# Hybrid encoder step on one core: feed-forward order, means of squares, transposed keys and first norm tiles

## The chip, the cores and the metric

The kernel runs on one NeuronCore of a Trainium2 chip. Its time is the device time of one launch in microseconds (us), as a median over runs. The engines have separate instruction queues and each works its queue in order: TensorE (PE) multiplies, VectorE (DVE) and ScalarE (ACT) work element by element and read the accumulators in PSUM, GpSimd (POOL) helps in SBUF and issues transfers, SyncE (SP) issues the weights' loads. Semaphores tie them together.

## What is computed

Two layers, on 512 prompt tokens and 32 sample tokens together (544 columns), in float32:

```python
x = x + 0.5 * swiglu(rms_norm(x, n1), f1a, f1b, f1c)        # ffn1
h = rms_norm(x, nm);  z = h @ w_in                          # mixing
...                  # branches: pooling (xp), stick-breaking attention (q, k, v with QK norm),
                     # spatial gating (gu, gv), gated linear attention (lq, lk, lv, la, lr)
merged = sum of sigmoid(gate_b) * (y_b @ w_branch[b]);  x = x + merged @ w_out
x = x + 0.5 * swiglu(rms_norm(x, n2), f2a, f2b, f2c)        # ffn2
x = x + sigmoid(rms_norm(x, npl) @ wpg) * (p_i @ wpp)       # ple
# swiglu(x, w1, w3, w2) = (silu(x @ w1) * (x @ w3)) @ w2;  1024 wide, 2816 hidden
```

Queries and keys are normed per head of 64 with the mean of their squares. The gated linear attention works in blocks of 128 tokens: scores from decayed queries and keys on six levels, masked into a matrix, and a state that is carried from chunk to chunk of 64.

## The kernel before

x and all activations lie transposed, channels on partitions, in 8 tiles of 128 x 544, each worked in two halves h of 272 columns. Every float32 product is three passes over a high and a low part (`mm`, line 391): high by high, low by high, high by low. A weight tile of 128 columns is loaded by SyncE, its high part cast on ScalarE (L157), its low part subtracted on VectorE (L161); `Weights.pump` (L196) makes the next one if one of 12 slots is free, and the low part of a job is issued with the following pump or when it is needed. Four PSUM tiles `pm` rotate for the projections, four `ps1` for side work.

The program is written in the order in which each queue gets it. A stage is a row of units; `unit` (L400) pumps, settles, runs its function and ticks. `settle` (L362) issues what was put off with `later`; `tick` (L278) lets side chains go one step each: pooling, the linear attention `gla_chain`, the query and key norms `post` (L1387), and others. A step that answers "wait" does not count.

The feed-forward stages: ffn1 of layer 0 is plain (`ffn`). The other three (`ffn7`, L703: ffn2 of both layers, ffn1 of layer 1) have a part 0 of four hidden tiles and three parts that use seven products for eight; for those, `PreNorm.combine` (L511) makes sums of norm blocks in 12 steps of a side chain. In these stages the norm is applied to x beforehand: `PreNorm.stats(h)` (L480) takes the mean of squares by a matmul, then a logarithm and an exponential on ScalarE; `normalise` (L491) makes y, the high part `nh` and the low part `nl` of a tile. `run_tail` (L549) runs the last projection of the stage ahead, in the order (0,0), (0,1), ..., (6,0), (7,0), (6,1), (7,1), and places statistics and norm tiles in it. `first` (L730) then multiplies three weight tiles at once, tile k by tile k of the norm, into three accumulators; half 1's statistics stand after k = 3. Before `ffn2` the tail is that of `w_out` (`o_unit`, L1770), one accumulator per unit; before ffn1 of layer 1 it is `ple` (L1779), two accumulators per unit and a tanh. `d_unit` (L850) is a down projection unit, which adds into x.

In the linear attention a block's step makes decays, settles, transposes the keys `k2` (L1173), scores levels 0 to 3, and yields; the next step has the states (L1082), scores of levels 4 and 5, and yields; the third has the diagonal and the next block's gates.

Of the kernel before, what the change touches and what calls it, by code (L numbers as in the profile page):

```python
# [220 lines left out]
def tile_encoder_step(ctx: ExitStack, tc: tile.TileContext, a, outs):  # L221
# [169 lines left out]
    def mm(ps, wh, pairs, h, first=True, last=True):  # L391
# [6 lines left out]
        W.used(wh)  # L398

    def unit(fn, ticks=1, pump=1):  # L400
        W.pump(pump)
        settle()
        fn()
        tick(ticks)


# [142 lines left out]
    def run_tail(n, fn, norm):  # L549

        order = [(m, h) for m in range(n - 2) for h in (0, 1)] + [(m, h) for h in (0, 1) for m in (n - 2, n - 1)]
        if isinstance(norm, PreNorm):
            for m, h in order[:-1]:
                unit(lambda: fn(m, h))
                if (m, h) == (7, 0):
                    later(norm.finish)
            norm.stats(0)
            W.pump(1)
            settle()
            norm.normalise(0, range(0, 2))  # L560
            fn(*order[-1])
            norm.normalise(0, range(2, 4))
            norm.finish()
            tick(1)
            norm.normalise(0, range(4, 8))
            return
        for m, h in order:
            unit(lambda: fn(m, h))
        if norm is not None:
            mid[:] = [0, norm.stats]  # L570
# [132 lines left out]
    def ffn7(p, x, norm, nxt, at_end=None):  # L703
# [26 lines left out]
        def first(h):  # L730

            tiles = [pm(), pm(), pm()]
            ws = [W.get(x) for x in (p1[0], p3[0], p1[1])]
            for k in range(8):
                xh, xl = norm.out[k]
                for ps, (hi, lo, o) in zip(tiles, ws):
                    for j, (w, z) in enumerate(((hi, xh), (lo, xh), (hi, xl))):
                        nc.tensor.matmul(ps, lhsT=w[:, k, o:o + 128], rhs=z[:, hs(h)], start=k == 0 and j == 0,  # L738
                                         stop=k == 7 and j == 2)
                if k == 3 and h == 0:  # L740
                    norm.stats(1)
            for x in (p1[0], p3[0], p1[1]):
                W.used(x)
            t = silu(tiles[0])
            t2 = silu(tiles[2])
            later(lambda: half_done(0, h, t, tiles[1]))
            return t2

        def product(ps, w, b, first=True):
# [5 lines left out]
            W.used(w)  # L755

        def unit7(fn, pump=1):
            settle()
            W.pump(pump)
            fn()  # L760
            tick()

# [56 lines left out]
        for part, (f0, nf) in enumerate(FF_PARTS7):  # L819
            last = part == len(FF_PARTS7) - 1  # L820
            if part == 0:
                for h in (0, 1):
                    settle()
                    t2 = first(h)
                    unit7(lambda: other(1, h, t2))
                    if h == 0:
                        norm.normalise(1, range(8))
                for f in range(2, nf):
                    if f == nf - 1:
                        c_sums = start(norm.combine(), front=True)  # L830
                    for h in (0, 1):
                        def f_unit():
                            ps = pm()
                            mm(ps, p1[f], norm.out, h)
                            t = silu(ps)
                            W.pump(1)
                            other(f, h, t)
                        unit7(f_unit)
# [11 lines left out]
            def d_unit(m, h):  # L850
                ps = pm()
                mm(ps, p2[part][m], [act[f] for f in range(f0, f0 + nf)], h)
                nc.vector.scalar_tensor_tensor(out=x[m][:, hs(h)], in0=ps, scalar=0.25, in1=x[m][:, hs(h)],  # L853
                                               op0=ALU.mult, op1=ALU.add)
# [5 lines left out]
            else:  # L860
                for m in range(8):
                    for h in (0, 1):
                        unit7(lambda: d_unit(m, h))
            act.clear()
# [71 lines left out]
    def mixing(L, v, x, norm, nxt):  # L936
# [119 lines left out]
        def gla_chain():  # L1056
# [57 lines left out]
            for i in range(5):  # L1114
# [57 lines left out]

                k2 = tt_("k2")  # L1173
                yield from need(1)
                ps = ps1()
                for f in range(2):
                    nc.tensor.transpose(ps[0:n, f * 128:(f + 1) * 128], ke[2 * f + 1][:, 2, :], ident)
                nc.scalar.copy(k2[0:n, 0:256], ps[0:n, 0:256])
                rel()

                att = st("att")
# [26 lines left out]
                yield  # L1208
                yield from states(i, n, nch, k2, bl, before, state)
                yield from scores((4, 5))  # L1210
                yield
                yield from need(2)
                banks = (ps1(), ps1())
# [159 lines left out]
        def qk_ep(dst, gain):  # L1373
            def ep(i, h, ps):
# [12 lines left out]
                def post():  # L1387
# [4 lines left out]
                    yield from need(1)  # L1392
                    settle()
                    p = ps1()
# [375 lines left out]
        def o_unit(m, h):  # L1770
            ps = pm()
            mm(ps, pl["w_out"][m], mpair, h)
            nc.vector.scalar_tensor_tensor(out=x[m][:, hs(h)], in0=ps, scalar=0.5, in1=x[m][:, hs(h)],
                                           op0=ALU.mult, op1=ALU.add)
            nxt.update(m, h)

        run_tail(8, o_unit, nxt)

    def ple(L, v, x, norm, nxt):  # L1779
# [3 lines left out]
        def fn(m, h):  # L1783
            pg, pp = pm(), pm()
            mm(pg, pg_w[m], norm.out, h)
            middle()
            t = norm.scale(pg, h)
            tanh(t, t, 0.5)
# [185 lines left out]
```

## Time and profile before

| what | value |
|---|---|
| median of 3 runs | 3130.62 us (3129.4 to 3132.0) |
| the profiled execution | 3129.3 us |
| its span, first to last instruction | 3127.5 us |
| TensorE busy | 3087.5 us, 99% of the span, 24432 matmuls |
| VectorE, ScalarE, GpSimd busy | 60%, 44%, 10% |
| DMA queues, largest share | 27.5% |

A busy share says that an engine had something in work, not that it had as much as it could take: matmuls overlap, and each is shown with its whole way through the array. So one looks for the places where TensorE has nothing: what a row names behind an arrow is what ended the idle time. Names such as nh, r, ke are the program's tiles, L738 is line 738.

### The profile page before, as it was taken

The page shows a single profiled execution, that of the slowest core. Times are in us where ns is not written, and L with a number is a line of the kernel's source. Part 1 is how long each engine was busy: PE and PEld are TensorE (multiplying, and loading weights), DVE is VectorE, ACT ScalarE, POOL GpSimd, SP SyncE. Part 2 cuts the span into 40 slices and gives each one's busy share as a digit, 9 for nine tenths or more (in the row PEclk, how much of TensorE's full clock was granted, in tenths as well). Part 3 has the DMA queues.
Part 4 walks back from the last instruction along what each step waited for, and adds up shares of the span by engine and source line. Part 5 has one row for each costly group of instructions (what it writes and reads, how often), then busy time and mean ns, then how long its engine had stood idle before and what let it go on. Part 6 is the DMA issues. An engine that isn't in the chain of part 4 may idle for free.

```text
span 3127.5 us, 58887 instructions
## 1 busy us (share of the span) xinstructions
PE 3087.5 (99%) x24432; PEld 3040.0 (97%) x24432; DVE 1863.2 (60%) x3766; ACT 1381.5 (44%) x2525; POOL 301.0 (10%) x393
## 2 busy tenths in 40 slices
PE   9999999999999999999999999999999999999999
PEld 8999999999999999999999999998999999999999
DVE  6444556766674557555666556477656654665564
ACT  4222334556664344334454334254666633443343
POOL 2000020101122000000300000111101221000000
PEclk9999999999999999999999999999999999999999
DMA  5232242224233322333323333422333233232331
GB/s 153 88 88 88 75 141 84 68 84 140 81 100 103 95 82 81 89 94 96 96 70 90 92 88 103 139 71 72 115 114 96 79 110 95 68 90 87 102 102 63
DMA packets 481387, 295.05 MB, mean 94 GB/s; under 512 B 13846, under 2 KB 466662, under 8 KB 481120
## 3 DMA queue, kind: packets, MB, share of 16 engines
q1 hardware_dynamic: 465440, 248.94, 27.5%
q0 software_dynamic: 11504, 34.55, 3.4%
q10 hardware_dynamic: 4176, 7.80, 0.7%
q8 instruction: 192, 3.15, 0.4%
q14 instruction: 75, 0.61, 0.1%
HBM read 270.41 MB, written 20.83 MB: 93 GB/s over the span
## 4 chain that ended last, share of the span: by engine, by line
PE 90%; DVE 6%; ACT 2%; issue 1%; DMA 0%; SPq 0%; ACTq 0%; DVEq 0%
PE pm L396 72%; PE pm L753 9%; PE pm L738 1%; DVE qe L1156 1%; PE ps L1662 1%; DVE lo L161 1%; PE ps L932 1%; PE ps L1653 1%; PE ps L1570 0%; PE ps L1196 0%; DVE sl L538 0%; ACT L340 0%; DVE ke L1147 0%; PE ps L1620 0%; PE ps L386 0%
## 5 line engine op out<-in xcount | busy, mean ns | idle before, releaser
L396 PE MATMUL pm<-nh,hi 128*128 128x272 f32 x4240 | 1237.3, 292 | 0.0
L396 PE MATMUL pm<-nh,lo 128*128 128x272 f32 x4240 | 1223.8, 289 | 2.7 <-DVE lo L161 2.7
L396 PE MATMUL pm<-nl,hi 128*128 128x272 f32 x4240 | 1221.7, 288 | 0.0
L396 PEld LDWEIGHTS pm<-nh,hi 128*128 128x128 f32 x4240 | 801.1, 189 | 7.8 <-issue 5.9
L396 PEld LDWEIGHTS pm<-nh,lo 128*128 128x128 f32 x4240 | 800.0, 189 | 3.1 <-DVE lo L161 2.9
L396 PEld LDWEIGHTS pm<-nl,hi 128*128 128x128 f32 x4240 | 801.1, 189 | 0.9
L157 ACT CAST hi<-raw 128x1024 fp32r<-128x1024 f32 (+1 forms) x434 | 436.1, 1005 | 214.8 <-PE pm L396 176.0
L161 DVE TENSOR_TENSOR lo<-raw,hi 128x1024 fp32r<-128x1024 f32 (+1 forms) x433 | 506.7, 1170 | 35.6 <-ACT hi L157 27.4
L396 PE MATMUL pm<-al,hi 128*128 128x272 f32 x1408 | 405.6, 288 | 2.7 <-DVE al L373 2.7
L396 PE MATMUL pm<-ah,hi 128*128 128x272 f32 x1408 | 406.4, 289 | 1.9 <-DVE x L853 1.9
L396 PE MATMUL pm<-ah,lo 128*128 128x272 f32 x1408 | 405.3, 288 | 0.0
L396 PEld LDWEIGHTS pm<-al,hi 128*128 128x128 f32 x1408 | 265.2, 188 | 3.4 <-DVE al L373 3.4
L396 PEld LDWEIGHTS pm<-ah,hi 128*128 128x128 f32 x1408 | 265.0, 188 | 2.9 <-DVE x L853 2.5
L455 DVE TENSOR_TENSOR u<-pm,r 128x272 f32<-128x272 f32 x296 | 129.9, 439 | 230.3 <-PE pm L396 223.9
L396 PEld LDWEIGHTS pm<-ah,lo 128*128 128x128 f32 x1408 | 264.9, 188 | 0.0
L375 ACT CAST ah<-sg 128x272 fp32r<-128x272 f32 x176 | 74.0, 420 | 309.5 <-DVE sg L677 107.5
L179 ACT CAST w<-raw 128x512 fp32r<-128x512 f32 x189 | 116.1, 619 | 204.9 <-DVE raw L176 155.7
L437 POOL TENSOR_TENSOR acc<-acc,sq 128x272 f32<-128x272 f32 x84 | 74.3, 884 | 1181.8 <-ACT sq L435 1181.8
L753 PE MATMUL pm<-sh,w 128*128 128x272 f32 x864 | 175.7, 288 | 0.0
L349 ACT ACTIVATE u<-u 128x272 f32<-128x272 f32 x160 | 69.0, 431 | 222.1 <-DVE u L455 221.9
L853 DVE SCALAR_TENSOR_TENSOR x<-pm,x 128x272 f32<-128x272 f32 x192 | 83.5, 437 | 115.1 <-PE pm L396 115.1
L396 PE MATMUL pm<-yh,lo 128*128 128x272 f32 x512 | 147.7, 288 | 0.0
(368 smaller groups left out, 4971.8 us busy)
## 6 DMA issues: line engine op xcount, KB each, us to landing
raw<-in_ffn_w_dram SPq DMA_DIRECT2D x204, 512.0 KB, 3.8
raw<-in_w_in_dram SPq DMA_DIRECT2D x136, 512.0 KB, 3.7
raw<-in_ffn_w_dram SPq DMA_DIRECT2D x80, 384.0 KB, 3.5
raw<-in_w_branch_dram SPq DMA_DIRECT2D x32, 512.0 KB, 3.4
raw<-in_w_out_dram SPq DMA_DIRECT2D x16, 512.0 KB, 4.0
raw<-in_ple_w_gate_dram SPq DMA_DIRECT2D x16, 512.0 KB, 4.0
yp<-park ACTq DMA_DIRECT2D x24, 272.0 KB, 4.4
park<-x POOLq DMA_DIRECT2D x16, 272.0 KB, 7.2
```

What stands on the lines that cost most here:

```text
L157: self.nc.scalar.copy(hi, src)
L161: (lower or self.nc.vector).tensor_tensor(out=lo, in0=src, in1=hi.bitcast(F32), op=ALU.subtract)
L179: self.nc.scalar.copy(hi, src)
L349: nc.scalar.activation(out, x, AF.Tanh, scale=scale)
L375: nc.scalar.copy(hi, src)
L396: nc.tensor.matmul(ps, lhsT=w[:, k, o:o + 128], rhs=x[:, hs(h)], start=first and k == 0 and j == 0, stop=last and k == n - 1 and j == 2)
L437: eng.tensor_tensor(out=self.acc[:, s], in0=self.acc[:, s], in1=q, op=ALU.add)
L455: nc.vector.tensor_tensor(out=out, in0=ps, in1=self.r[:, hs(h)], op=ALU.mult)
L738: nc.tensor.matmul(ps, lhsT=w[:, k, o:o + 128], rhs=z[:, hs(h)], start=k == 0 and j == 0, stop=k == 7 and j == 2)
L753: nc.tensor.matmul(ps, lhsT=u[:, j, :], rhs=z, start=first and j == 0 and i == 0, stop=j == 3 and i == 2, skip_group_check=not first)
L853: nc.vector.scalar_tensor_tensor(out=x[m][:, hs(h)], in0=ps, scalar=0.25, in1=x[m][:, hs(h)], op0=ALU.mult, op1=ALU.add)
L932: nc.tensor.transpose(ps[0:n, g * 128:(g + 1) * 128], s[:, t0:t0 + n], ident)
```

## The change

Norm: `run_tail` gives the first statistics and the first two norm tiles of the next feed-forward stage to a hook that `o_unit` and `ple` call right after a unit's first matmuls, ahead of that unit's update of x; four more tiles stand ahead of the last unit, two behind it. The table for logarithms is loaded ahead of the tail of `w_out`. `first` also fetches the fourth weight, and half 1's first four tiles stand before the first product's activation. Feed-forward: the combination of norm blocks begins one hidden tile earlier and gets a second step per unit; `d_unit` settles after its first matmuls; the down projections of part 0 pump in every second unit, of later parts not in their first; the tails use `unit7`, which settles before it pumps. Mixing: `post` no longer settles before the mean of squares; `k2` and its copy stand in the second step, before the scores of levels 4 and 5, and the states open the third.

```diff
--- before.py
+++ after.py
@@ -397,11 +397,24 @@
                                  start=first and k == 0 and j == 0, stop=last and k == n - 1 and j == 2)
         W.used(wh)

+    hook = []
+
+    def hooked():
+
+        if hook:
+            hook.pop()()
+
     def unit(fn, ticks=1, pump=1):
         W.pump(pump)
         settle()
         fn()
         tick(ticks)
+
+    def unit7(fn, pump=1):
+        settle()
+        W.pump(pump)
+        fn()
+        tick()


     class Norm:
@@ -551,21 +564,24 @@
         order = [(m, h) for m in range(n - 2) for h in (0, 1)] + [(m, h) for h in (0, 1) for m in (n - 2, n - 1)]
         if isinstance(norm, PreNorm):
             for m, h in order[:-1]:
-                unit(lambda: fn(m, h))
+                if (m, h) == (6, 1):
+                    def begin():
+                        norm.stats(0)
+                        norm.normalise(0, range(0, 2))
+                    hook.append(begin)
+                unit7(lambda: fn(m, h))
                 if (m, h) == (7, 0):
                     later(norm.finish)
-            norm.stats(0)
+            settle()
+            norm.normalise(0, range(2, 6))
             W.pump(1)
-            settle()
-            norm.normalise(0, range(0, 2))
             fn(*order[-1])
-            norm.normalise(0, range(2, 4))
             norm.finish()
             tick(1)
-            norm.normalise(0, range(4, 8))
+            norm.normalise(0, range(6, 8))
             return
         for m, h in order:
-            unit(lambda: fn(m, h))
+            unit7(lambda: fn(m, h))
         if norm is not None:
             mid[:] = [0, norm.stats]

@@ -730,7 +746,7 @@
         def first(h):

             tiles = [pm(), pm(), pm()]
-            ws = [W.get(x) for x in (p1[0], p3[0], p1[1])]
+            ws = [W.get(x) for x in (p1[0], p3[0], p1[1], p3[1])]
             for k in range(8):
                 xh, xl = norm.out[k]
                 for ps, (hi, lo, o) in zip(tiles, ws):
@@ -739,6 +755,8 @@
                                          stop=k == 7 and j == 2)
                 if k == 3 and h == 0:
                     norm.stats(1)
+            if h == 0:
+                norm.normalise(1, range(0, 4))
             for x in (p1[0], p3[0], p1[1]):
                 W.used(x)
             t = silu(tiles[0])
@@ -753,12 +771,6 @@
                     nc.tensor.matmul(ps, lhsT=u[:, j, :], rhs=z, start=first and j == 0 and i == 0,
                                      stop=j == 3 and i == 2, skip_group_check=not first)
             W.used(w)
-
-        def unit7(fn, pump=1):
-            settle()
-            W.pump(pump)
-            fn()
-            tick()

         def pair(f):
             q = p1[f]
@@ -824,9 +836,9 @@
                     t2 = first(h)
                     unit7(lambda: other(1, h, t2))
                     if h == 0:
-                        norm.normalise(1, range(8))
+                        norm.normalise(1, range(4, 8))
                 for f in range(2, nf):
-                    if f == nf - 1:
+                    if f == nf - 2:
                         c_sums = start(norm.combine(), front=True)
                     for h in (0, 1):
                         def f_unit():
@@ -834,6 +846,7 @@
                             mm(ps, p1[f], norm.out, h)
                             t = silu(ps)
                             W.pump(1)
+                            tick()
                             other(f, h, t)
                         unit7(f_unit)
             else:
@@ -850,6 +863,8 @@
             def d_unit(m, h):
                 ps = pm()
                 mm(ps, p2[part][m], [act[f] for f in range(f0, f0 + nf)], h)
+                if (m, h) == (0, 0):
+                    settle()
                 nc.vector.scalar_tensor_tensor(out=x[m][:, hs(h)], in0=ps, scalar=0.25, in1=x[m][:, hs(h)],
                                                op0=ALU.mult, op1=ALU.add)
                 if last:
@@ -860,7 +875,7 @@
             else:
                 for m in range(8):
                     for h in (0, 1):
-                        unit7(lambda: d_unit(m, h))
+                        unit7(lambda: d_unit(m, h), h if part == 0 else 1 if m or h else 0)
             act.clear()

     def col_vec(dst, src, n):
@@ -1170,14 +1185,6 @@
                 lg = lgs[i] = None
                 settle()

-                k2 = tt_("k2")
-                yield from need(1)
-                ps = ps1()
-                for f in range(2):
-                    nc.tensor.transpose(ps[0:n, f * 128:(f + 1) * 128], ke[2 * f + 1][:, 2, :], ident)
-                nc.scalar.copy(k2[0:n, 0:256], ps[0:n, 0:256])
-                rel()
-
                 att = st("att")
                 nc.vector.memset(att[0:n, 0:4 * n], 0.0)
                 att3 = att[0:n, 0:4 * n].rearrange("p (h t) -> p h t", h=4)
@@ -1206,9 +1213,17 @@

                 yield from scores((0, 1, 2, 3))
                 yield
+
+                k2 = tt_("k2")
+                yield from need(1)
+                ps = ps1()
+                for f in range(2):
+                    nc.tensor.transpose(ps[0:n, f * 128:(f + 1) * 128], ke[2 * f + 1][:, 2, :], ident)
+                nc.scalar.copy(k2[0:n, 0:256], ps[0:n, 0:256])
+                rel()
+                yield from scores((4, 5))
+                yield
                 yield from states(i, n, nch, k2, bl, before, state)
-                yield from scores((4, 5))
-                yield
                 yield from need(2)
                 banks = (ps1(), ps1())
                 for f in range(2):
@@ -1390,7 +1405,6 @@
                     yield "wait"
                     yield "wait"
                     yield from need(1)
-                    settle()
                     p = ps1()
                     mean(p[:, 0:HT], bd64, sq)
                     r = tt_("r")
@@ -1770,10 +1784,12 @@
         def o_unit(m, h):
             ps = pm()
             mm(ps, pl["w_out"][m], mpair, h)
+            hooked()
             nc.vector.scalar_tensor_tensor(out=x[m][:, hs(h)], in0=ps, scalar=0.5, in1=x[m][:, hs(h)],
                                            op0=ALU.mult, op1=ALU.add)
             nxt.update(m, h)

+        ln_set()
         run_tail(8, o_unit, nxt)

     def ple(L, v, x, norm, nxt):
@@ -1784,6 +1800,7 @@
             pg, pp = pm(), pm()
             mm(pg, pg_w[m], norm.out, h)
             middle()
+            hooked()
             t = norm.scale(pg, h)
             tanh(t, t, 0.5)
             mm(pp, pp_w[m], ppair, h)
```

## Rows read from the trace of the kernel before

**Rows 1.** The page, its first line.
```profile
span 3127.5 us, 58887 instructions
```

**Rows 2.** Waits of TensorE: who, releaser: us in total, times, longest.
```profile
PE pm L738 <- ACT nh L502: 7.0, 6, 1.3
PE ps L1196 <- ACT r L380: 6.3, 4, 2.9
PE ps L1177 <- DVE ke L1147: 3.7, 2, 1.9
PE pm L396 <- DVE al L373: 2.7, 3, 0.9
PE pm L396 <- DVE lo L161: 2.7, 1, 2.7
PE pm L396 <- DVE x L853: 1.9, 3, 0.7
```

**Rows 3.** Chain of waits: start us, us, what, matmuls.
```profile
973.52 142.84 PE pm L396 x1140
```

**Rows 4.** Windows: stretch, us, busy by engine, granted clock, DMA share, GB/s.
```profile
634.00:644.00 10.00, 7.14 (x56) 6.51 (x57) 4.80 (x14) 3.98 (x6) 1.47 (x4) 0.83 0.23 67
2078.00:2085.00 7.00, 6.84 (x46) 6.31 (x43) 4.59 (x12) 1.83 (x5) 1.58 (x3) 0.76 0.32 101
```

**Rows 5.** Timeline, TensorE: start us, us, what, count, idle before.
```profile
1116.19 0.62 PE L485 MATMUL ps<-acc,m 128*128 128x272 f32 x2
```

**Rows 6.** Timeline, ScalarE, the same stretch.
```profile
1117.31 1.28 ACT L340 ACT_TABLE_LOAD   x1
1118.61 0.49 ACT L380 ACTIVATE r<-ps,eps 128x272 f32<-128x272 f32 x1
```

**Rows 7.** Timeline, VectorE, the same stretch.
```profile
1119.59 0.80 DVE L501 TENSOR_TENSOR y<-x,r 128x272 f32<-128x272 f32 x2 [2.76 <-ACT r L381]
...
1122.13 0.78 DVE L501 TENSOR_TENSOR y<-x,r 128x272 f32<-128x272 f32 x2
...
1123.99 0.43 DVE L474 TENSOR_TENSOR acc<-acc,sq 128x272 f32<-128x272 f32 x1
```

**Rows 8.** Timeline, TensorE, start of the first product, layer 0.
```profile
1120.97 0.39 PE L738 MATMUL pm<-nh,hi 128*128 128x272 f32 x1 [1.14 <-ACT nh L502]
```

**Rows 9.** Timeline, TensorE, start of the first product, layer 1's ffn1.
```profile
1573.81 0.39 PE L738 MATMUL pm<-nh,hi 128*128 128x272 f32 x1 [1.10 <-ACT nh L502]
...
1575.11 0.39 PE L738 MATMUL pm<-nh,hi 128*128 128x272 f32 x1
```

**Rows 10.** Timeline, VectorE, the same stretch.
```profile
1574.62 0.43 DVE L455 TENSOR_TENSOR u<-pm,r 128x272 f32<-128x272 f32 x1
```

**Rows 11.** Timeline, TensorE, the product after it.
```profile
1588.54 0.39 PE L396 MATMUL pm<-nh,lo 128*128 128x272 f32 x1 [2.67 <-DVE lo L161]
```

**Rows 12.** Timeline, VectorE, down projection of part 0.
```profile
1175.07 0.43 DVE L373 TENSOR_TENSOR al<-sg,ah 128x272 fp32r<-128x272 f32 x1
```

**Rows 13.** Timeline, TensorE, linear attention's fourth block, layer 0.
```profile
634.17 0.68 PE L1096 MATMUL ps<-lvt,k 64*64 64x128 f32 x16
...
638.12 1.29 PE L1196 MATMUL ps<-qe,ke 128*128 128x128 f32 x6 [2.86 <-ACT r L380]
```

**Rows 14.** Timeline, ScalarE, the same stretch.
```profile
635.30 0.43 ACT L1381 ACTIVATE sq<-q 128x272 f32<-128x272 f32 x1 [3.61 <-DVE q L455]
```

**Rows 15.** Timeline, TensorE, linear attention's first block, layer 0.
```profile
525.43 0.33 PE L1177 MATMUL ps<-ident,ke 128*128 128x128 f32 x1 [1.88 <-DVE ke L1147]
```

**Rows 16.** Timeline, VectorE, the same block.
```profile
523.51 1.27 DVE L1156 TENSOR_TENSOR qe<-e,lq 64x64 f32<-64x64 f32 x8
...
531.08 1.68 DVE L1204 COPY_PREDICATED att<-masks,ps 128x128 f32<-128x128 uint8 x8
```

**Rows 17.** Timeline, TensorE, the same block's end.
```profile
534.60 0.37 PE L396 MATMUL pm<-nh,hi 128*128 128x272 f32 x1
```

**Rows 18.** Timeline, VectorE, the second block.
```profile
565.07 1.68 DVE L1204 COPY_PREDICATED att<-masks,ps 128x128 f32<-128x128 uint8 x8
```

More of the change, by code (lines that the diff above doesn't have):

```diff
@@ L1208, in gla_chain @@
                 yield
-                yield from states(i, n, nch, k2, bl, before, state)
+                k2 = tt_("k2")
[5 more added lines that the diff above has]
+                rel()
                 yield from scores((4, 5))
                 yield
+                yield from states(i, n, nch, k2, bl, before, state)
                 yield from need(2)
```

## Prediction

> **What bounds the kernel now.** I read the page first: the span is 3127.5 us [rows 1] and TensorE (PE) is busy for nearly all of it, so time can only come from its stops, from its clock, or from fewer matmuls; the change takes none away. Next the waits of TensorE [rows 2]: six kinds of stop, 7.0 + 6.3 + 3.7 + 2.7 + 2.7 + 1.9 = 24.3 us, are at places that the diff touches. In a long undisturbed piece of the chain of waits a matmul takes 142.84 / 1140 = 0.125 us [rows 3], while one counts as busy for 0.29, so each stop costs some 0.16 us more than its idle time. Last the granted clock [rows 4]: the stretch after the long stop at 638 us has 0.83 over 10 us, that at 2078 us 0.76 over 7 us; both times 1.7 us are lost, some 3.4 us at the lower level (1.2 GHz) after TensorE stood still. There are four such stretches, two in each layer's mixing stage, with 0.72 to 0.83 in windows of 6 to 10 us. The profiled execution took 3129.3 us, 1.8 around its span, and the median is 3130.6; what I take from the trace I subtract from the median.
>
> **Norm tiles at the feed-forward stages with the seven-product form (three: ffn2 of layer 0, ffn1 and ffn2 of layer 1).** Before, in ffn2 of layer 0, the sums' matmul runs at 1116.19 for 0.62 us [rows 5], yet ScalarE (ACT) starts the logarithm at 1118.61, behind a square and a table load of 1.28 [rows 6]. Tiles 0 and 1 are built from 1119.59 [rows 7] and the first product stops 1.14 us for them at 1120.97 [rows 8], 1.30 with the hidden part. After: the table is loaded before the stage, the sums come ahead of the square, so the logarithm starts near 1116.9, its root is there 0.98 later (1118.61 to 1119.59), and both tiles long before they are needed at 1119.67. That stop goes. What is late next: six tiles now stand ahead of the last update of x on VectorE (DVE), not two. Two tiles take 1.86 us, from 1122.13 to the operation after them at 1123.99 [rows 7], four 3.65. So: 1117.9 + 1.86, update of x for tile 6 (0.35), + 3.65, then the last update at 1123.7, its square after a weight cast on ACT, and the sum of squares complete at 1125.2. TensorE wants it for the second half's statistics after half of the first product, 36 matmuls from 1119.67, at 1124.2: a new stop of 1.0. Against 1.30 and some 0.6 in small waits for low parts before, 0.9 gained. The second half's tiles, which started behind a weight split and made the next product stop 1.30 idle, 1.46 in all (in the 7.0 of rows 2), now begin before the first product ends: 1.45 gained. **2.35 for each ffn2, 4.7 for both.**
>
> In ffn1 of layer 1 the stage ahead takes two accumulators per unit, and the first product's third accumulator is that of unit (7, 1): before, it started at 1575.11 [rows 9], right when the scaling that reads the old content ended (1574.62 + 0.43 [rows 10]). After, that scaling stands behind four more tiles: 1569.2 (root ready) + 1.86 + unit 6's epilogue with its tanh table (to 1573.2) + 3.65 = 1576.9, so the third accumulator starts at 1577.4 instead of 1573.3: a new stop of 4.1, against 3.6 lost there before (idle 1.10 at 1573.81 [rows 9], another 1.0, small ones). But the stop of 2.67 for a weight's low part at 1588.54 [rows 11] goes, since the fourth weight is now fetched ahead of the product. Net 2.25; with a chance of a half-clock stretch behind a 4 us stop (1.7 at 6 in 10) **1.25**. Bounds for this row, which the trace of before cannot show: 6.5 gained if the accumulator comes free early, 2 lost if weights also queue ahead of it. I take the low middle, as the order of the instructions on VectorE is fixed by the program.
>
> **Feed-forward order, three stages.** Before, two stops in the down projection of part 0: for a low part at 1175.07 behind two operations of the sums' combination (0.9 idle, three times in 2.7 [rows 2]), and for an accumulator as VectorE falls behind (0.6, three in 1.9). With the refill (0.16 each) 5.5 us. After: the low part is settled before the first update of x (it would start near 1172.9, before the update that began at 1173.4; it is needed at 1174.5 and came at 1175.07 [rows 12]), and eight of the twelve combination steps now lie in the up projection, at two per 6 us unit: VectorE has there 3 x 0.35 + 2 x 1.13 of splits + 2 x 1.1 = 5.5 of 6 us. That cover is thin, but accumulators have a unit of slack. The down projection's 8 units of weight pumping instead of 16 cost nothing: splits there are held by slots, nine in all, and eight pumps and one before suffice. The settle put before the pump in the tails only swaps neighbours on VectorE. **5.5 gained**, bounds 1 lost (5.5 becomes 6 with one more split per unit) and 5.5.
>
> **Squares' means without the settle.** At 634.78 the scores of levels 4 and 5 start; their second bank waits until 638.12, 2.86 us [rows 13], for the logarithm that reads the older mean. That stands on ACT behind the square of the newest unit, which VectorE let in only at 635.30 after 3.61 us of idle ACT [rows 14], then the cast and a table load of 1.28. Without the settle the load runs at 631.7, the logarithm right after its mean at 633.9. Also the rotation of four banks moves by the key transposes, and the scores no longer take that bank. 2.86 + 0.15, the half-clock stretch of 1.7 [rows 4], and 0.3 at the last block, times two layers: **10 gained**. The states' 16 matmuls, 0.68 us [rows 13], are only moved. Bounds: nothing (another reader of a bank ends as late) and 10.6.
>
> **Transposed keys behind scores.** The stop at 525.43, 1.88 us, is for keys that VectorE makes last [rows 15]. The scores want the eight products before: 523.51 + 1.27 [rows 16], of which the first level's end about 524.4; TensorE idles from 523.55 for 0.85. So 1.15 is won, and lost again: the later scores now take the banks of the earlier ones, whose eight masked copies run from 531.08 to 532.76 [rows 16] because VectorE is behind with the decayed products; nothing in the change moves them. TensorE arrives at 530.1 and waits 2.6. The projection that began at 534.60 [rows 17] begins at 533.55, and the states (0.7) are still to come: 0.3 net, 0.5 in layer 1. At the second block the copies end at 566.75 [rows 18], as late as TensorE's next group did, 0.7 lost; at the third 0.5 won. Sum over two layers: **0.4**; bounds 5 lost (half-clock after each wait) and 5.4 (all 2.0 + 0.7 per layer).
>
> The Trainium skill, TensorE: Matmul & The Clock Gate, Terms, puts the loss at the throttled time times one minus the ratio. By it each of the four stretches is worth 1.7 wherever it lies, 6.8 for all, and the gain would be 3.4 larger, 3106 us. The rows agree on the size, but in block 0 of layer 0 the masked copies end at 532.76 whatever TensorE does in between, so there I count nothing.
>
> Sum: 4.7 + 1.25 + 5.5 + 10 + 0.4 = 21.9, less 1 for small waits that a new bank order brings: 21 us. 3130.6 - 21 = **3109.6 us**.
>
> **Rivals.**
> 1. Nothing comes in place of the stops: 24.3 + 19 x 0.16 (3.0) + three stretches of clock (5.1) = 32.4, 3098 us. For it: each stop's releaser is moved. Against it: rows 10 and 16 show VectorE late whatever the order.
> 2. The settle was not what held the logarithm: the bank stop stays, 10 less, 3120 us. Against it: ACT's idle 3.61 before the square [rows 14]. For it: a weight cast can stand there too.
> 3. Six tiles ahead of the last update cost what they give: both ffn2 win nothing and layer 1's ffn1 loses 2 with the clock, 5.95 + 2 less, 3118 us.
> 4. Slower. The later scores depend on banks of the earlier ones in all ten blocks. If VectorE is as late in each as in the first (2.6 us, plus 1.7 of half clock), 10 x 4.3 = 43 against 21 + 0.4: 3152 us. It decides from 2.1 us per block on. For it: rows 16 and 18. Against it: at the fourth block the copies end at 633.4, when TensorE gets there, and the last block is small. The Trainium skill, Perfetto Trace Analysis, Optimization Strategy, says that the same gap repeating can mean too little PSUM for the next tile; by it this rival would show ten like waits, where the trace of before has two.
> 5. It does nothing to the time that counts: 3130 us.
>
> **How the numbers follow.** Forecast 52 in 100 (own range 3104 to 3116), rival 1 15, rival 2 12, rival 3 14, rival 4 4, rival 5 3. The range 3096 to 3122 takes in the forecast, rivals 2 and 3, and 1 at its edge: their terms' bounds leave about 2 in 10 outside. A measurement of this kernel tells 0.2%, 6.3 us, from no change. Faster by more: 92; within it 4; slower 4.
>
> **What would show it.** Right: no stop for r at the scores of the fourth block; half-clock stretches at 638 and 2184 gone; no stop for al or x in the down projections; a new stop of 1 us for acc at the statistics of ffn2 and of 4 us for u in layer 1's ffn1; waits of later scores for att in the first blocks. Wrong: a stop for r still there, waits for att of over 2 us in most blocks, or no new stops at all and some 3098 us.

## Result and profile after

| what | before | after |
|---|---|---|
| median of four runs | 3130.99 us (3129.4 to 3132.0) | 3108.98 us (3108.9 to 3109.3) |
| the profiled execution, its span | 3129.3, 3127.5 | 3109.03, 3107.3 |
| TensorE busy, matmuls | 3087.5, 24432 | 3076.9, 24432 |

The ratio is 0.9932, with a 95% interval of 0.992 to 0.9944: 22 us faster where 21 were forecast. The span's row answers to [rows 1]:

```profile
span 3107.3 us, 58862 instructions
```

The waits of TensorE in the changed kernel answer to [rows 2] (who, releaser: us in total, times, longest):

```profile
PE ps L1203 <- DVE att L1211: 4.8, 4, 1.9
PE pm L754 <- DVE u L468: 4.1, 1, 4.1
PE ps L498 <- DVE acc L487: 2.3, 2, 1.2
PE ps L1203 <- DVE qe L1171: 1.7, 2, 0.8
PE ps L1221 <- ACT yq L1026: 1.1, 2, 0.6
```

None of the six kinds of [rows 2] is left: 24.3 us of stops went, and 14.0 came in the five kinds shown. All of TensorE's idle time, its span less its busy time, fell from 40.0 to 30.4 us, so about half of the 20.2 us that the span lost is idle time; the rest lies in matmuls that follow each other more closely. Both kernels have 24432 matmuls, so the start of the k-th can be compared between the traces; that shows where the time went, stage by stage, with everything that refilling the array after a stop and the clock add (k and us):

```
k        start before    after minus before    what lies since the row above
 3900        508.7            +0.2             start of the launch, up to the first block
 4800        627.5            +1.8             layer 0, blocks 1 to 3: transposed keys
 5100        668.4            -3.4             layer 0, blocks 4 and 5: squares' means
 8700       1117.9            -3.2
 8900       1146.7            -5.3             layer 0, ffn2: norm tiles
 9500       1224.1            -7.6             its up and down projection: order
12250       1569.8            -8.5             (0.9 over 345 us, no single place)
12400       1595.2            -8.2             layer 1, ffn1: norm tiles
13000       1672.5           -10.4             order
16100       2064.1           -10.3
16900       2171.2           -11.9             layer 1, blocks 1 to 3: transposed keys
17200       2212.6           -17.1             layer 1, blocks 4 and 5: squares' means
20600       2636.5           -16.5
21000       2690.6           -18.6             layer 1, ffn2: norm tiles
21500       2755.4           -20.6             order
24431       3123.5           -20.3
```

As terms: norm tiles in ffn2 2.1 + 2.1, in ffn1 -0.3, order 2.3 + 2.2 + 2.0, squares' means 5.1 + 5.2, transposed keys -1.5 + 1.6; with the drifts between them 20.3, which is the difference of the two profiled executions.

The granted clock of the two stretches of [rows 4], then of two new ones, then of layer 1's fourth block (columns as there):

```profile
634.00:644.00 10.00, 9.90 (x92) 8.77 (x91) 6.75 (x22) 6.02 (x13) 1.47 (x4) 1.00 0.24 67
2070.00:2077.00 7.00, 6.92 (x65) 5.93 (x65) 3.36 (x9) 4.36 (x8) 0.71 (x2) 1.00 0.40 117
533.00:543.00 10.00, 9.92 (x76) 8.93 (x77) 5.71 (x14) 4.52 (x10) 1.58 (x3) 0.83 0.25 80
1567.00:1574.00 7.00, 4.88 (x21) 4.88 (x22) 5.43 (x13) 4.77 (x8) 0.00 (x0) 0.52 0.00 0
2170.00:2200.00 30.00, 29.90 (x257) 27.86 (x256) 19.93 (x72) 18.56 (x45) 4.38 (x10) 1.00 0.27 76
```

Layer 0's fourth block runs at the full clock now, and so does layer 1's first, where [rows 4]'s second stretch was (some 10 us earlier in time now); layer 1's fourth block, 0.76 from 2183 to 2190 us in the kernel before, does too. Layer 0's first block has a half-clock stretch (0.83 over 10 us: 3.4 us at 1.2 GHz), and layer 1's ffn1 nearly 7 us of one around its long stop. Five rows of TensorE's timeline (start, us, what, count, idle before) show the new stops of both places; the first answers to [rows 15], the second and third to no row of before, the fourth to [rows 9] and the last to [rows 5, 8]:

```profile
524.74 0.35 PE L1203 MATMUL ps<-qe,ke 128*128 128x128 f32 x1 [0.84 <-DVE qe L1171]
...
530.58 0.33 PE L1221 MATMUL ps<-ident,ke 128*128 128x128 f32 x1 [0.58 <-ACT yq L1026]
...
532.95 0.42 PE L1203 MATMUL ps<-qe,ke 128*128 128x128 f32 x1 [1.93 <-DVE att L1211]
...
1569.12 0.59 PE L754 MATMUL pm<-nh,hi 128*128 128x272 f32 x1 [4.12 <-DVE u L468]
...
1122.31 0.70 PE L498 MATMUL ps<-acc,m 128*128 128x272 f32 x2 [1.17 <-DVE acc L487]
```

And ScalarE in the fourth block, for [rows 14]: the table is loaded 2.6 us ahead of the logarithm, which starts right behind its mean.

```profile
633.18 1.28 ACT L340 ACT_TABLE_LOAD   x1
635.81 0.49 ACT L380 ACTIVATE r<-ps,eps 128x272 f32<-128x272 f32 x1 [1.35 <-PE ps L386]
```

### The profile page after: what moved, and what is told of

Read it like the earlier page. It is cut to its first block, busy times and chain, and to the rows that moved or that the text cites. A ratio compares the mean times of both kernels' runs of the same rounds, so it can differ in the third digit from the quotient of the medians.

```text
span 3107.3 us, 58862 instructions
## 1 busy us (share of the span) xinstructions
PE 3076.9 (99%) x24432; PEld 3034.4 (98%) x24432; DVE 1857.9 (60%) x3766; ACT 1383.3 (45%) x2525; POOL 318.3 (10%) x393
## 4 chain that ended last, share of the span: by engine, by line
PE 94%; DVE 4%; ACT 1%; issue 1%; DMA 0%; SPq 0%; ACTq 0%; DVEq 0%
PE pm L396 75%; PE pm L771 9%; PE pm L754 2%; DVE qe L1171 1%; PE ps L1676 1%; PE ps L947 1%; PE ps L1667 1%; PE ps L1584 0%; PE ps L1203 0%; PE ps L386 0%; DVE lo L161 0%; PE ps L1634 0%; PE ps L1633 0%; DVE att L1211 0%; PE ps L1561 0%
## 5 line engine op out<-in xcount | busy, mean ns | idle before, releaser
L450 POOL TENSOR_TENSOR acc<-acc,sq 128x272 f32<-128x272 f32 x84 | 92.4, 1099 | 1167.9 <-ACT sq L448 1167.9
L396 PE MATMUL pm<-yl,hi 128*128 128x272 f32 x512 | 147.6, 288 | 0.0
```

The lines of the kernel that those rows point to most:

```text
L396: nc.tensor.matmul(ps, lhsT=w[:, k, o:o + 128], rhs=x[:, hs(h)], start=first and k == 0 and j == 0, stop=last and k == n - 1 and j == 2)
L450: eng.tensor_tensor(out=self.acc[:, s], in0=self.acc[:, s], in1=q, op=ALU.add)
```

## Experiments

The first four each undo one part of the change.

**The settle ahead of the mean, put back.**

```diff
                     yield from need(1)
+                    settle()
                     p = ps1()
                     mean(p[:, 0:HT], bd64, sq)
```

> The changed kernel (3109.0 us) with only the settle ahead of the mean of squares put back. Theory: the settle alone sets how late ScalarE takes the logarithm, so the stop for r at the scores of the fourth block returns in both layers with its half-clock stretch, 5.1 us a layer: 3119 us, and the matmuls' start times fall back by about 5 us at 640 and at 2180 us and nowhere else. Rival: it was the moved key transposes, which turn the rotation of the four banks so that these scores no longer need the bank of r; then nothing returns there and the time is 3109 to 3110 us. A time of 3112 to 3116 us would mean that each gives a part.

Measured 3116.1 us (3114.6 to 3119.4), 7.1 more than the changed kernel; ratio to before 0.9956 (0.9941 to 0.997). ScalarE stands still for 3.88 us as in [rows 14], and the logarithm is late again; TensorE, though, stops for r at the diagonal, for 1.0 us, not at the scores for 2.9 as in [rows 13] (ScalarE, then TensorE, then the clock behind the stop):

```profile
638.12 0.43 ACT L1396 ACTIVATE sq<-q 128x272 f32<-128x272 f32 x1 [3.88 <-DVE q L468]
...
639.02 1.28 ACT L340 ACT_TABLE_LOAD   x1
640.32 0.49 ACT L380 ACTIVATE r<-ps,eps 128x272 f32<-128x272 f32 x1
```

```profile
643.69 0.67 PE L1232 MATMUL ps<-lq,lk 64*128 64x128 f32 x4 [1.01 <-ACT r L380]
```

```profile
642.00:652.00 10.00, 8.99 (x54) 7.05 (x45) 5.00 (x13) 4.31 (x10) 1.47 (x4) 0.66 0.16 44
```

So both are true. The settle makes the logarithm late; the moved transposes turn the rotation of four banks, and the late bank is met by another instruction, with a stop 1.9 us shorter. A second stop follows in the fifth block, 0.98 us for att, so not all of the 1.9 is saved. A half-clock stretch of 6.8 us (0.66 over 10) lies behind the stop of only 1.0. Layer 1 has the same stop of 1.01 at its diagonal, and no stretch behind it: by the matmuls' starts the settle costs 5.9 us in layer 0 and 2.7 in layer 1. This profiled execution is the slowest of the four, 3119.4 us.

**The key transposes and states, put back.**

```diff
+                k2 = tt_("k2")
+                ...
                 att = st("att")
 ...
                 yield from scores((0, 1, 2, 3))
                 yield
-                k2 = tt_("k2")
-                ...
+                yield from states(i, n, nch, k2, bl, before, state)
                 yield from scores((4, 5))
                 yield
-                yield from states(i, n, nch, k2, bl, before, state)
```

> The changed kernel with the key transposes back ahead of the first scores and the states back ahead of the scores of levels 4 and 5. Theory: the waits for the masked copies go and the wait for the last keys returns, and the two cancel over the two layers, because in both VectorE's queue of decayed products sets the end: 3109 us, within 1.5. In layer 0 1.5 us should be won (the half-clock stretch behind the new waits goes too), in layer 1 1.6 lost. Rival: the moved transposes give what their old stop cost, some 2.5 us a layer, and the losses seen are chance: 3114 us. Second rival: the stop for r returns at the fourth block because the bank rotation is the old one: 3119 us.

Measured 3108.5 us (3107.5 to 3109.4), -0.5: nothing. The stops for ke are back, as in [rows 2]; those for att and qe at the scores are gone, and two shorter ones a layer stand at the states instead (0.45 and 0.54 us in layer 0). No stop for r appears: without the settle the old rotation is as good.

```profile
PE ps L1192 <- DVE ke L1162: 3.7, 2, 1.9
```

By the matmuls' starts layer 0 wins 1.5 us in blocks 1 to 3 and layer 1 loses 0.1; the profiled execution has no half-clock stretch in either first block.

**The norm tiles, put back** (the tail, half 1's tiles, the fourth weight and the table load as in the kernel before; the tails keep `unit7`).

> The changed kernel with the norm tiles where they were: statistics of half 0 behind the last unit but one, two tiles ahead of the last unit, half 1's tiles behind the second product, no fourth weight ahead, no table load ahead of the tail. Theory: the stops for nh and for nl return in both ffn2 (2.1 us each, as the matmuls' start times show) and in layer 1's ffn1 nothing is lost or 0.3 won, for the stop of 4.1 us and its half-clock stretch go and the old stops come back: 3109.0 + 4.2 - 0.3 = 3113 us. Rival: six tiles cost what they give also in ffn2: 3109 us. Second rival: the fourth weight alone carries ffn1, so that 2.7 us more are lost: 3116 us.

Measured 3113.2 us (3111.6 to 3116.2), +4.2. The waits for nh and for a low part are back, about as in [rows 2]; u and acc are gone.

```profile
PE pm L751 <- ACT nh L515: 6.9, 6, 1.3
PE pm L396 <- DVE lo L161: 2.6, 1, 2.6
```

By the matmuls' starts the two ffn2 lose 2.1 and 2.0, and ffn1 of layer 1 wins 0.3.

**The feed-forward order, put back.**

```diff
-                    if f == nf - 2:
+                    if f == nf - 1:
 ...
-                            tick()
                             other(f, h, t)
 ...
-                if (m, h) == (0, 0):
-                    settle()
 ...
-                        unit7(lambda: d_unit(m, h), h if part == 0 else 1 if m or h else 0)
+                        unit7(lambda: d_unit(m, h))
```

> The changed kernel with the feed-forward order put back: combination one hidden tile later and one step a unit, no settle behind the first matmuls of the down projection, a weight pumped in every unit of it. Theory: the stops for al and for x return at the down projection of part 0 in three stages, 2.2 us each as the matmuls' start times show: 3109.0 + 6.6 = 3115.6 us. Rival: the combination's steps are only moved under the up projection, and VectorE's queue costs there what it saved: 3109 to 3111 us.

Measured 3117.0 us (3114.9 to 3118.2), +8.0; al and x stop TensorE three times each, as in [rows 2], and cost 2.3, 2.1 and 2.1 us by the matmuls' starts.

```profile
PE pm L396 <- DVE al L373: 2.7, 3, 0.9
PE pm L396 <- DVE x L865: 1.9, 3, 0.7
```

The profiled execution (3114.9 us) is 5.8 slower than that of the changed kernel: these 6.5, a half-clock stretch of layer 1's first block that the changed kernel's lacks (1.6), less the one of layer 0's first block that this one lacks (1.6), and some 0.7 of launch and drift. It is the fastest of the four; what makes their median 2.1 us longer is not shown. The four parts undone singly give 18.8 of the 22.0.

These stretches need a word, since one alone moves a time by some 1.6 us; they may be part of the spread of the medians, but one execution of each kernel was profiled, so that is not shown. Seven kernels, the changed one among them, have the same first blocks, with the same stops of 0.84, 0.58 and 1.93 us; their profiled executions show a half-clock stretch there in layer 0 five times and in layer 1 six times, each worth some 1.5 to 1.6 us by the matmuls' starts. So these stops alone do not settle whether a stretch comes. The changed kernel's profiled execution has the one and not the other; its four runs lie within 0.4 us.

The next ones take the new stops apart.

**The last unit first.** VectorE's order in the tail is changed: the last unit's accumulator is read ahead of tiles 2 and 3, and the sum of squares completed within tiles 4 and 5.

```diff
             settle()
-            norm.normalise(0, range(2, 6))
+            hook2.append(lambda: norm.normalise(0, range(2, 4)))
+            fn(*order[-1])
+            norm.normalise(0, range(4, 8), norm.finish)
             W.pump(1)
-            fn(*order[-1])
-            norm.finish()
             tick(1)
-            norm.normalise(0, range(6, 8))
 ...
             mm(ps, pl["w_out"][m], mpair, h)
             hooked()
+            hooked(hook2)
 ...
             mm(pp, pp_w[m], ppair, h)
+            hooked(hook2)
```

> The changed kernel (3109.0 us) with another order in the tail ahead of the three norm stages: the last unit's reading of its accumulator comes first on VectorE (in the tail with two accumulators the scaling u, in the other only tiles 2 and 3 stand ahead of the update of x), then tiles 2 and 3, the last unit's update, and the last sum of squares between tiles 4 and 5. Theory: the stop of 4.1 us in layer 1's ffn1 is VectorE's order and nothing else, and the half-clock stretch is its follower, so 3.6 + 3.4 us go there and 1.3 us at the statistics of each ffn2: 3109.0 - 9.6 = 3099.4 us. Rival: VectorE has no room, tiles 2 to 4 come late instead and stop the product by 0.5 to 1 us each: 3104 to 3106 us, with stops for nl or nh in place of u and acc. Second rival: the half-clock stretch comes whatever the stop: 3102.8 us.

Measured 3107.6 us (3104.8 to 3108.5), -1.4: a miss of 8 us. The stops for u (4.1 to 0.2) and acc went as expected, and at ordinal 12300 the matmul is 5.5 us earlier than in the changed kernel; at 12420 only 1.0 is left. The next product waits for the activation, which now queues behind half 1's four tiles on both engines (TensorE, then ScalarE, then two windows of the clock):

```profile
1580.51 0.39 PE L755 MATMUL pm<-nh,hi 128*128 128x272 f32 x1 [2.46 <-DVE sg L358]
```

```profile
1577.76 0.52 ACT L515 ACTIVATE nh<-y,norm_ffn 128x272 fp32r<-128x272 f32 x1 [0.24 <-DVE y L514]
1578.30 1.28 ACT L349 ACT_TABLE_LOAD   x1
1579.59 0.69 ACT L349 ACTIVATE sg<-pm 128x272 f32<-128x272 f32 x2
```

```profile
1566.00:1576.00 10.00, 10.00 (x77) 9.79 (x78) 7.93 (x18) 7.02 (x14) 1.03 (x1) 1.00 0.05 13
1580.00:1590.00 10.00, 9.49 (x64) 9.49 (x65) 5.51 (x14) 3.94 (x8) 0.00 (x0) 0.83 0.01 2
```

The half-clock stretch at 1567 us was the stop's follower, then, and came back with the next stop. The profiles of all seven kernels that have the stop of 4.1 us for u show a stretch with it, 6.8 us long in six and 3.4 in the one with the settle put back.

**The activation between half 1's tiles**, on top of it.

```diff
             if h == 0:
-                norm.normalise(1, range(0, 4))
+                norm.normalise(1, range(0, 2))
 ...
             later(lambda: half_done(0, h, t, tiles[1]))
+            if h == 0:
+                settle()
+                norm.normalise(1, range(2, 4))
             return t2
```

> The kernel of the last unit first (3107.6 us), and in the first product of the three norm stages two of half 1's tiles, not four, stand ahead of the activation; the activation's work on VectorE follows, then tiles 2 and 3. Theory: what kept 8 of the 9.6 us from coming was the next thing late, the activation's two accumulators behind half 1's tiles on VectorE and ScalarE: a stop of 2.5 us with a half-clock stretch (0.83 over 10 us, 1.7) in layer 1's ffn1 and 0.65 in each ffn2. With two tiles ahead the accumulators come 1.6 us earlier: the stop falls to about 0.9 without the stretch, and those of ffn2 go: 3107.6 - 1.6 - 1.7 - 1.5 = 3102.8 us. Rival: tiles 2 and 3 of half 1 then come too late for the second product, with stops for nh or nl of the same size: 3107 us.

Measured 3103.3 us (3102.9 to 3103.7), 4.2 less. The stop for sg is 0.7, in one place, and the stretch from 1580 to 1590 has a granted clock of 1.00. By the matmuls' starts ffn1 gains 3.4 us more than with the last unit first alone, and the two ffn2 0.9 and 1.0 more. So the stop in ffn1 was VectorE's and ScalarE's order, one late instruction behind the other.

**Three weights.** Only the fourth weight's early fetch is taken out of the changed kernel.

```diff
-            ws = [W.get(x) for x in (p1[0], p3[0], p1[1], p3[1])]
+            ws = [W.get(x) for x in (p1[0], p3[0], p1[1])]
```

> The changed kernel with only the fourth weight no longer fetched ahead of the first product. Theory: the stop for a weight's low part behind the first product of layer 1's ffn1 (2.67 us before the change) returns, since the low part again waits for VectorE behind half 1's tiles: 3109.0 + 2.8 = 3111.8 us. Rival: the stop of 4.1 us ahead of it gives VectorE and ScalarE the time to make that weight anyway, and nothing returns: 3109 us.

Measured 3115.6 us (3114.5 to 3116.9), +6.6. The stop returns at 3.5 us, longer than [rows 11], with a clock of 0.83 in the 10 us behind it:

```profile
1583.39 0.44 PE L396 MATMUL pm<-nh,lo 128*128 128x272 f32 x1 [3.54 <-DVE lo L161]
```

Across ffn1's first products the matmuls fall back by 5.3 us (the rest is the first blocks' stretches, one gone and one come, and the start of the launch). So within the changed kernel this one line is worth 5.3 us in layer 1's ffn1, with the stretch behind the stop, and the tiles' order loses a little more than that.

**The later scores in the third step.**

```diff
                 rel()
-                yield from scores((4, 5))
                 yield
                 yield from states(i, n, nch, k2, bl, before, state)
+                yield from scores((4, 5))
```

> The changed kernel with the scores of levels 4 and 5 moved from the second step of a block, behind the key transposes, to the third, behind the states. Theory: these scores wait for the masked copies only because they come one unit after the earlier scores; a unit later the copies are long done, the waits for att (2.5 us a layer) go and with them the half-clock stretch in layer 0: 3109.0 - 5.0 - 1.7 = 3102.3 us. Rival: with states, scores and diagonal in one step five banks' worth of work stands in a row, and the diagonal waits for the state updates in all ten blocks, 0.5 to 0.8 us each: 3107 to 3110 us.

Measured 3108.5 us (3107.4 to 3109.3), -0.5: a miss. The waits for att at these scores went and others came: 3.6 us for k at the states (four times, up to 1.0) and 1.9 at the transposes for the values (eight of 0.2). The copy of k stands on ScalarE behind work that waits for VectorE: in layer 0's first block it starts at 534.42 us, right behind two operations the first of which had waited 1.35 us for VectorE's u. The two edits together, the last unit first and these later scores:

> The last two edits together. Theory: they touch different stages, so the gains add: 3109.0 - 9.6 - 6.7 = 3092.7 us, or what the two single runs give as a sum. Rival: none beyond those of the two; if the sum does not hold, a stage couples to the next by more than its matmuls.

Measured 3106.2 us (3103.7 to 3106.7): the sum of the two measured gains (1.4 + 0.5) would be 3107.1, which lies within the spread.

**Work moved from VectorE to GpSimd.**

```diff
-                            (nc.vector if f else nc.gpsimd).tensor_tensor(out=k3, ...)
+                            nc.gpsimd.tensor_tensor(out=k3, ...)
 ...
-                nc.vector.memset(att[0:n, 0:4 * n], 0.0)
+                nc.gpsimd.memset(att[0:n, 0:4 * n], 0.0)
```

> The changed kernel (3109.0 us), with the decayed keys of the second head pair (two operations of 0.69 and 0.56 us a block) and the clearing of the score matrix (0.48) on GpSimd in place of VectorE. Theory: the waits of the first blocks (qe 0.84, att 1.93 and 0.48 a layer) are VectorE's lateness, which no order of the chain's steps has removed; with 1.7 us less on VectorE the masked copies of the first block end 1.5 us earlier, the wait for att falls from 1.93 to about 0.4 and that for qe from 0.84 to 0.5, in layer 0 with its half-clock stretch (1.7): 3109.0 - 2 x 2.2 - 1.7 = 3102.9 us. Rival: VectorE's queue is filled again at once by the gating's work and the copies come no earlier, or GpSimd, which takes 1.3 and 1.0 us for the same two operations, makes the keys late: 3109 us or more, with waits for ke.

Measured 3108.3 us (3108.0 to 3109.3), -0.7: a miss of 5 us. The wait for att fell (4.8 to 1.2 us in all), and that for qe rose from 0.84 to 2.1. The timelines of GpSimd and of VectorE in the first block show why:

```profile
522.80 2.52 POOL L1162 TENSOR_TENSOR ke<-e,lk 128x512 f32<-128x512 f32 x2 [2.83 <-DVE df L1015]
525.26 0.52 POOL L1189 MEMSET att<- 128x512 f32 x1
```

```profile
523.15 3.03 DVE L1171 TENSOR_TENSOR qe<-e,lq 64x64 f32<-64x64 f32 x7
```

Eight of these VectorE operations take 1.27 us in [rows 16]; here seven take 3.03, because the two that start beside GpSimd's two products last until those end (1.29 and 1.02 us in place of 0.21, each ending 0.07 behind its product). During the clearing they take 0.21 to 0.23. The Trainium skill, SBUF — State Buffer, SBUF: two separate sides, says that VectorE and GpSimd share a pair of ports as an exclusive lock, held for the whole instruction, and that a VectorE operation with two SBUF inputs meets it only against a GpSimd operation that reads SBUF; the trace agrees on both counts, the clearing reading nothing.

**Only the clearing on GpSimd**, with the last unit first and the activation between; then the same with the later scores.

> The kernel with the activation between half 1's tiles (3103.3 us), and of the last experiment only the clearing of the score matrix (0.48 us a block) on GpSimd; the decayed keys stay on VectorE. Theory: a VectorE operation with two operands in SBUF that starts beside a GpSimd operation of the same kind ends only with it, which is why the moved keys made qe late; a clearing on GpSimd held no VectorE operation. So the masked copies of the first blocks come 0.48 us earlier at no price: waits for att 0.5 less in the first two blocks of each layer, 3103.3 - 1.9 = 3101.4 us. Rival: clearing holds VectorE too, or VectorE's queue is filled at once by the gating's work: 3103 us.

Measured 3097.4 us (3095.5 to 3099.7); ratio to before 0.9898 (0.9881 to 0.9914). The longest wait for att fell from 1.9 to 1.2, those of the second block went, and the half-clock stretch of the first block with them:

```profile
PE ps L1207 <- DVE att L1215: 2.3, 2, 1.2
```

```profile
533.00:543.00 10.00, 9.92 (x91) 8.94 (x90) 6.38 (x17) 6.30 (x13) 1.58 (x3) 1.00 0.27 82
```

Compared with the kernel that has all but the clearing, the matmuls gain 2.2 us in layer 0's first block, 1.5 in its next two and 2.3 in layer 1's three: 6.0 in all, three times the 1.9 expected. Of this, 1.6 is the half-clock stretch that layer 0's first block no longer has, which the expectation left out, and 2.5 is less waiting for att (4.8 to 2.3 us); the rest is not taken apart. By the medians it is 5.9, but the kernel before was 1.3 us faster beside this run than beside the kernel without the clearing, which leaves 4.6. Its layer 1 still has a stretch in the first block. With the later scores too:

> The same kernel with the scores of levels 4 and 5 in the third step as well. Theory: in the first blocks the order of the steps only chooses which wait shows VectorE's lateness, so the time is that of the kernel without this edit, within 1 us (the same edit took 0.5 us from the changed kernel and 1.3 us from the one with the last unit first): 3100.5 to 3101.5 us. Rival: with copies 0.5 us earlier the later order no longer waits for k either, and 2 us more are won: 3099.4 us.

Measured 3098.3 us (3097.9 to 3098.5), the same, and with a spread of 0.6 us where the kernel without it had 4.2: none of the four kernels without those waits for att at the later scores shows a half-clock stretch in a first block. That this narrows the spread is not shown: the other three of them spread by 1.9 to 3.0 us. Both versions beat the changed kernel by some 11 us, and the one before by 31 to 32.

## Why the prediction was right, point by point

- **Norm tiles, ffn2.** Right in mechanism and place: the first stop gone, the new one 1.17 us for acc where 1.0 was worked out; 4.2 gained of 4.7.
- **Norm tiles, layer 1's ffn1.** The stop was forecast at 4.1 us for u, and is 4.12. The gain was -0.3 in place of 1.25: the failing step is the price of the half clock, 1.7 us at 6 in 10. It came, from 1567.3 to 1574.1, and the 20 matmuls in it after the stop took 0.23 us each, not 0.126: 2.1 us, where 1.0 had been set. By the Trainium skill, TensorE: Matmul & The Clock Gate, Terms, those 6.8 us at half speed would cost an estimated 3.4; the trace has less, since 1.8 of them lie in the stop, when TensorE had nothing to do. With the settle put back the stretch is 3.4 us and the same stage gains 0.7. The clock makes 1.1 of the 1.55 that are missing; where the other 0.45 went stays open. The term rested on a difference of larger ones: within the changed kernel the fourth weight alone is worth 5.3.
- **Feed-forward order.** Right: no stop for al or x left, 6.5 gained of 5.5. That VectorE's cover holds was seen too: nothing new waits in the up projections.
- **Squares' means.** Right in size, 10.3 for 10, stop, half clock and last block. With the keys put back no stop for r is left either, and the matmuls of these blocks lose nothing, so taking out the settle is enough for all of it. The new rotation by itself gives less: with the settle put back 7.1 are lost again by the medians. The prediction named the rotation and did not price it.
- **Transposed keys.** 0.1 for 0.4, right as a sum, in the mechanism (VectorE's first masked copies end at 533.0 us, with the launch 0.2 later, where 532.76 stood) and for qe's 0.85. Wrong inside: layer 0 lost 1.5 and layer 1 won 1.6, the latter because the stretch of its first block stayed away, as it did in one of the seven kernels alone. The sum owes that to luck, and without it would be some 1.5 lost. The stop of 0.58 for a bank still read by the pooling's copy (yq) was not seen. The wait for att was 1.93 where 2.6 stood, because TensorE came later, by that stop for the most part.
- **Rivals.** Rival 1 falls, since five new stops came. Rival 2 falls with the settle put back, rival 3 with the tiles put back, though its second half (ffn1 gains nothing) holds. Rival 4's mechanism is there, with 1.9 us in the first block, 0.5 in the second and nothing over 0.2 later, so it doesn't decide. Rival 5 falls with the 22 us, far outside the interval.

Left open: why the same stops in the first blocks bring a half-clock stretch in one kernel and not in another; and up to 1.6 us in the first 35 us of the launch, which differ between executions.

## What to carry to other kernels

Where one engine is late, its order only chooses which instruction waits: price a moved step by what is late next, and the one after that, since each new stop can bring the half clock with it. Take work off the late engine before its order is changed again; but look at what the other engine's instruction reads, or it gives the time back. Where both kernels have the same number of matmuls, compare the start of the k-th in both traces: it prices each part of a change at once.

## What the runs showed of the hardware

- A GpSimd product of 1.0 to 1.6 us holds a VectorE operation of 0.21 until it ends; a GpSimd clearing of 0.52 does not. The kernel before pays this as well, in each of its first three blocks: VectorE's first eight qe operations of the block take 3.2 us beside GpSimd's ke, the next eight, alone, 1.27 [rows 16]. The timelines of GpSimd and VectorE in the kernel before:

```profile
516.54 2.26 POOL L1147 TENSOR_TENSOR ke<-e,lk 128x512 f32<-128x512 f32 x2 [8.94 <-ACT e L1131]
```

```profile
516.59 3.21 DVE L1156 TENSOR_TENSOR qe<-e,lq 64x64 f32<-64x64 f32 x8
```

- A half-clock stretch lies behind a stop as short as 1.0 us in one layer, and none behind the same stop in the other (the settle put back); one of 6.8 us began 2.3 us into a stop of 4.1 (the changed kernel).
